# A planned encoder-layer kernel: nine instead of eight projection pairs by seven half products, in another order

## The chip, the core and the metric

The kernel runs on one core of a Trainium2 chip, as one program. The metric is the device time of one execution in microseconds (us). Before the change three runs took 727.42, 727.95 and 728.01 us; the median is 727.95. One further execution was profiled, and its trace gives all the durations used here.

A core has engines that run side by side, each with its own instruction stream: TensorE (PE; its weight loads are told apart as PEld), VectorE (DVE), ScalarE (ACT), GpSimd (POOL) and SyncE (SP, which only issues transfers). Sixteen DMA engines move the data.

## The reference: one encoder layer

Everything is float32. `x` has 512 tokens of 1024 features. The layer computes, with weights of some 68 MB in all:

```python
proj = x @ w_in                          # 1024 x 3840
qa, ka, va, qb, kb, vb = split(proj)     # 16 q heads, 4 k and v heads of 64; then 12 + 12 + 12
qa, ka, qb, kb = rope(...)               # first 16 of 64 dimensions turned by position
o_a = windowed attention(qa, ka, va)     # |i - j| <= 128, a sink logit per head, blocks of 128 queries
o_b = dilated mixture(qb, kb, vb)        # three groups of 4 heads: dilation 1, 4, 16; merged by softmax weight
g_a, g_b = sigmoid(x @ w_gate + b_gate)  # 1024 x 2048
y = (g_a * (o_a @ w_br_a) + g_b * (o_b @ w_br_b)) @ w_out
h = layer_norm(a * x + y)
out = layer_norm(a * h + (silu(h @ w_ff_gate) * (h @ w_ff_up)) @ w_ff_down)   # 1024 x 2816, twice, and back
```

## The kernel before

**Precision.** A float32 product is made of three fast products. Each operand is split into a high part (a cast) and a low part (the value less the high part); high x high, high x low and low x high are added in PSUM. So each 128-row slice of weights costs a load, a cast (on ACT or DVE, `cp_alts` or `copy_by_act`) and a subtraction on DVE, before TensorE takes three products.

**Dense units.** A unit is 128 output features: 8 slices of 128 inputs, three products of 512 columns each, 24 in all (`feat_x`, lines 523 to 525). Its weights come as two halves of 256 KB.

**Pairs.** `pair_x(ua, ub)` computes two units at once by Strassen's scheme in Winograd's form: seven products of half size instead of eight. The weights of both units form a 2 x 2 block matrix; blocks A11, A12 and A22 are loaded, S1 and S3 are loaded as sums (a plain load on SP's queue, and a second transfer on GpSimd's queue that adds to it), S2 and S4 are formed on DVE. All seven are split. The forms T1 to T4 of x are made once (`x_forms`, token `X`). Each product is 4 slices x 3 products of 256 columns (lines 639 to 641), so a pair has 84. ScalarE and VectorE take the results out of the banks.

**The planner.** Nothing is issued in the order of the text. `op(...)` notes an operation with what it reads and writes, the engines that can do it and a reckoned duration. `Program.run` then simulates all engines and at each moment gives a free engine the operation of lowest priority value whose inputs are there and whose buffers fit; this gives each engine's instruction order, which the chip then runs with semaphores. A priority is `pr.T`, the TensorE time noted so far, plus an offset: -130 for weights (`LOOK`), -100 for results out of banks (`EV`), so weights are sought 130 us ahead. `limits` counts buffers: 85 slots of 256 KB in classes (general, weights, attention), 8 PSUM banks, and `unit`, how many attention units may be under way at once. `SPARE` slots are kept free for the operation that is first in line.

**The order.** `ORDER` is a list of tokens. `VA` are the values of mixer A, `q1` to `q3` dense units of its queries, `P:a,b` a pair, `g` a gate, `R` turns the heads just computed by position (16 rows of each are gathered by DMA, four VectorE operations, and sent back), `A0` to `A3` the attention of mixer A (four blocks each), `Q00`, `K00` ... queries and keys of mixer B (head pair, group), `V0` and `V12` its values, `B0` to `B3` its four head slots, `O` fetches a slice of mixer A's output, `L` changes the weight buffers' limits, `X` makes the forms of x. Two gates are computed along with the first units.

**Gates.** There are 16; numbers 8 to 15 belong to mixer B and are computed first. `gate` makes one by a dense unit, `gate_of` takes one from a pair. `AWAY` holds 8 to 15: those made by a pair are stored in DRAM after the tanh (`put_away`) and fetched again after the last exponential of B3 (`fetch_gate`). `gate` does not store, so that gates 8 to 10 stay in their slots.

**After it.** When attention ends, the two branch products follow in the order `BRANCHES` (a0 to a4, b0, a5, ...), `gated` (line 1413) multiplies by the gates, then come the output product, the first layer norm, 22 blocks of the feed-forward net by half products (lines 1690 to 1692), its way back (1901 to 1903) and the last layer norm.

## Time and profile before

| what | value |
|---|---|
| median of three runs | 727.95 us (727.42 to 728.01) |
| span of the profiled execution | 725.8 us |
| TensorE busy | 717.3 us (99%) |
| VectorE busy | 655.6 us (90%) |
| ScalarE busy | 471.4 us (65%) |
| GpSimd busy | 134.0 us (18%) |
| moved by DMA | 140.3 MB, 193 GB/s |

The span goes from the first to the last instruction; the profile gives no other time for this execution, and the median of the runs is 2.15 us above it. A row of a group of instructions reads: line, engine, operation, what it writes `<-` what it reads (`sl` a slot, `ps` a PSUM bank, `x` the split x, `wpack` the weights, `gz` a gate in DRAM), shape, count | busy us, mean ns of one | idle time before them and who ended it. A row of the timeline reads: start in us, duration, engine, line, operation. Matmuls overlap: the duration of one is longer than the distance to the next.

### The profile page before, as it was taken

How to read it: one execution, taken by the hardware profiler on the slowest of the kernel's cores; microseconds unless marked ns; L12 is line 12 of the kernel's file. 1: busy time of each engine (PE TensorE's matmuls, PEld its weight loads, DVE VectorE, ACT ScalarE, POOL GpSimd, SP SyncE). 2: the span in 40 equal slices, each digit the busy share in tenths (PEclk: the TensorE clock that was granted, in tenths of full speed). 3: DMA queues.
4: the chain of work that ended last, by engine and by line, in shares of the span. 5: the costliest groups of instructions: out<-in, count | busy, mean ns of one | idle time of the engine just before them, and what ended most of it. 6: DMA issues, size and time to landing. Idle time of an engine off the chain costs nothing.

```text
span 725.8 us, 14412 instructions
## 1 busy us (share of the span) xinstructions
PE 717.3 (99%) x4767; PEld 666.2 (92%) x4767; DVE 655.6 (90%) x1408; ACT 471.4 (65%) x1077; POOL 134.0 (18%) x297
## 2 busy tenths in 40 slices
PE   9999999999999999999999999999999999999995
PEld 7889999989988888988888999999999999999985
DVE  6999999889997898898967898899999999899987
ACT  5757798868778665666534666756666566666821
POOL 0021211111100731450020021111112211212000
PEclk9999999999999999999999999999999999999998
DMA  8978788856577689965681499676888888979302
GB/s 256 309 155 202 191 213 246 211 135 172 170 192 185 160 228 253 309 217 185 216 209 44 116 267 228 154 199 155 200 254 212 193 215 225 258 184 200 97 30 87
DMA packets 88010, 140.30 MB, mean 193 GB/s; under 512 B 11136, under 2 KB 24064, under 8 KB 87936
## 3 DMA queue, kind: packets, MB, share of 16 engines
q1 hardware_dynamic: 74336, 114.87, 51.7%
q0 software_dynamic: 13328, 24.39, 20.5%
q8 instruction: 37, 0.61, 0.3%
q14 instruction: 37, 0.30, 0.1%
q10 hardware_dynamic: 272, 0.13, 0.1%
HBM read 114.97 MB, written 7.60 MB: 169 GB/s over the span
## 4 chain that ended last, share of the span: by engine, by line
PE 99%; DVE 1%; DVEq 0%; issue 0%
PE ps L1692 10%; PE ps L1691 9%; PE ps L1690 9%; PE ps L523 9%; PE ps L524 9%; PE ps L525 9%; PE ps L1901 4%; PE ps L1903 4%; PE ps L1902 4%; PE ps L641 3%; PE ps L640 3%; PE ps L639 3%; PE ps L973 3%; PE ps L1480 3%; PE ps L1481 3%; PE ps L1482 3%
## 5 line engine op out<-in xcount | busy, mean ns | idle before, releaser
L373 ACT ACTIVATE sl<-sl 128x512 fp32r<-128x512 f32 (+3 forms) x419 | 230.8, 583 | 59.7 <-DVE sl L544 31.1
L544 DVE TENSOR_TENSOR sl<-sl,sl 128x512 fp32r<-128x512 f32 (+3 forms) x378 | 222.4, 621 | 5.1 <-ACT sl L373 3.4
L373 ACT ACTIVATE sl<-ps 128x256 f32<-128x256 f32 (+5 forms) x209 | 88.7, 445 | 91.6 <-PE ps L1692 56.8
L387 POOL DMA_DIRECT2D sl<-wpack x60 | 53.1, 885 | 342.9 <-DMA sl<-wpack 118.2
L1691 PE MATMUL ps<-sl,sl 128*128 128x256 f32 x352 | 96.8, 275 | 0.0
L1692 PE MATMUL ps<-sl,sl 128*128 128x256 f32 x352 | 96.8, 275 | 0.0
L1690 PE MATMUL ps<-sl,sl 128*128 128x256 f32 x352 | 96.8, 275 | 0.0
L523 PE MATMUL ps<-x,sl 128*128 128x512 f32 (+1 forms) x241 | 93.9, 389 | 0.0
L525 PE MATMUL ps<-x,sl 128*128 128x512 f32 (+1 forms) x241 | 91.4, 379 | 0.0
L524 PE MATMUL ps<-x,sl 128*128 128x512 f32 (+1 forms) x209 | 79.5, 380 | 0.0
L1690 PE MATMUL ps<-x,sl 128*128 128x256 f32 x264 | 72.6, 275 | 0.0
L1691 PE MATMUL ps<-x,sl 128*128 128x256 f32 x264 | 72.6, 275 | 0.0
L1692 PE MATMUL ps<-x,sl 128*128 128x256 f32 x264 | 72.6, 275 | 0.0
L1691 PEld LDWEIGHTS ps<-sl,sl 128*128 128x128 f32 x352 | 67.6, 192 | 0.1
L1690 PEld LDWEIGHTS ps<-sl,sl 128*128 128x128 f32 x352 | 67.6, 192 | 0.1
L1692 PEld LDWEIGHTS ps<-sl,sl 128*128 128x128 f32 x352 | 67.6, 192 | 0.0
L399 DVE TENSOR_TENSOR sl<-sl,sl 128x512 fp32r<-128x512 f32 x94 | 62.8, 682 | 1.8 <-ACT sl L373 1.3
L525 PEld LDWEIGHTS ps<-x,sl 128*128 128x128 f32 x241 | 45.9, 190 | 6.5
L1690 PEld LDWEIGHTS ps<-x,sl 128*128 128x128 f32 x264 | 50.6, 192 | 0.4
L1691 PEld LDWEIGHTS ps<-x,sl 128*128 128x128 f32 x264 | 50.6, 192 | 0.4
L523 PEld LDWEIGHTS ps<-x,sl 128*128 128x128 f32 x241 | 46.0, 191 | 5.4 <-ACT sl L373 0.3
L1692 PEld LDWEIGHTS ps<-x,sl 128*128 128x128 f32 x264 | 50.7, 192 | 0.0
(172 smaller groups left out, 1851.0 us busy)
## 6 DMA issues: line engine op xcount, KB each, us to landing
sl<-wpack SPq DMA_DIRECT2D x249, 256.0 KB, 3.9
sl<-wpack POOLq DMA_DIRECT2D x60, 256.0 KB, 5.3
sl<-sl SPq DMA_DIRECT2D x110, 128.0 KB, 3.1
wf<-wpack SPq DMA_DIRECT2D x51, 256.0 KB, 5.2
wf<-wpack POOLq DMA_DIRECT2D x24, 256.0 KB, 6.2
oa<-sl SPq DMA_DIRECT2D x32, 128.0 KB, 3.6
sl<-sl SPq DMA_DIRECT2D x68, 32.0 KB, 2.6
sl<-oa SPq DMA_DIRECT2D x8, 256.0 KB, 5.1
```

The source lines that it names most:

```text
L373: nc.scalar.activation(dst, src, AF.Copy)
L387: op([(POOL, 1.0)], lambda e: nc.gpsimd.dma_start(b.t, src2, accum_op=ALU.add), reads=[b], writes=[b], prio=prio, moves=1.65)
L399: op([(DVE, dve(S))], lambda e: nc.vector.tensor_tensor(l.t, src.t, f32(h.t), op=ALU.subtract), reads=[src, h], writes=[l], prio=prio, abs ...
L523: mm(o, a, x0, start=(k == 0 and begins), stop=False, skip_group_check=split)
L524: mm(o, a, x1, start=False, stop=False, skip_group_check=split)
L525: mm(o, b, x0, start=False, stop=(k == nk - 1), skip_group_check=split)
L544: op([(DVE, dve(w))], lambda e: nc.vector.tensor_tensor(dst(), x(), y(), op=o), reads=reads, writes=writes, prio=prio)
L1690: mm(o, wh, pairs(bh[k]()), start=(first and k == 0), stop=False, skip_group_check=True)
L1691: mm(o, wh, pairs(bl[k]()), start=False, stop=False, skip_group_check=True)
L1692: mm(o, wl, pairs(bh[k]()), start=False, stop=(k == 3), skip_group_check=True)
L1901: mm(ps.t, x0, pairs(w[0].t), start=(first and m == 0), stop=False, skip_group_check=True)
L1902: mm(ps.t, x0, pairs(w[1].t), start=False, stop=False, skip_group_check=True)
```

## The change

One more pair: `Q10` and `K11`, dense units before, are computed by seven half products. The tokens of `ORDER` stand in another order, the other pairs are made of other units, and each token can carry an offset `@n` that is added to its priorities. Queries and keys are looked up by number, since they are no longer made in order. `gate` stores gates 8 to 15 in DRAM as well, so all eight go that way. Three attention units instead of two may be under way, ten instead of twelve slots are kept spare, the forms of x and the second values unit are ranked otherwise, and four fetches of mixer A's output wait for B1 instead of B0. The planner reckons the time until a transfer has landed 1.3 times as long as before, up to 380 us, and a transposition of four blocks 0.436 instead of 0.36 us.

The change also brings code that no token of the order calls: sums of a pair formed by DMA (`D:`), rows turned by DMA alone (`r`), values of mixer B by half products (`V`, `half_values`, `PV`) and sums of `unit_b` by DMA (`SUM_BY_DMA`, empty).

```diff
-SPARE, SPARE2 = 12, 12
+SPARE, SPARE2 = (10, 12)
...
-UNITS = 2
+UNITS = 3
...
+LONG = 1.3
...
 ORDER = """
-VA q1 A0 q2 q3 g X P:k1,q4 R A1 P:q5,g P:q6,q7 R A2 P:g,g A3 P:g,g L P:Q00,K00 R V12 P:Q01,K01 R P:Q02,K02 R V0 B0 Q10 K10 R Q11 K11 R B1 O O Q12 K12 R O O B2 B3 O O O O g8
+VA@-157 q2@22 q3@-17 g@46 X@-31 P:q6,q7@32 q1@-321 P:k1,q5@-23 R@-23 A1@-1 P:q4,Q02@-22 R@-13 V12@4 A0@-104 P:Q01,g@-19 A2@42 P:Q00,K00@8
+A3@-15 P:g,g@9 R@80 P:g,K01 R@-38 L@-65 P:g,K02 V0@33 R@2 P:Q10,K11@-27 R@-4 K10@1 Q12@-10 B0@-51 Q11@-32 B1@-2 O@11 R@-204 K12@-21 O@26 g@32
+R@31 O@-117 O@-34 g@-6 g@-45 g@-32 g@-9 B2@-102 O@-23 O@-77 g@-21 g@-1 B3@-47 g@-42 O@-172 O@-3
 """
-FORMS = -60.0
-VAL = -100.0
-OA_AFTER = (0, 0, 0, 0, 0, 0, 0, 0)
+FORMS = -135.0
+VAL = -130.0
+OA_AFTER = (0, 0, 0, 1, 1, 1, 0, 1)
...
+SUM_BY_DMA = ()
...
-                        o.done = moved + (LATE if 95 < now < 150 else 2.4 if 14 < now < SLOW else 0.87)
+                        o.done = moved + (LONG if now < 380 else 1.0) * (LATE if 95 < now < 150 else 2.4 if 14 < now < SLOW else 0.87)
...
-                        o.done = moved + (0.87 if e == ACT else 6.2 if ACC < now < 420 else 3.2 if 14 < now < SLOW else 2.2)
+                        o.done = moved + (LONG if now < 380 else 1.0) * (0.87 if e == ACT else 6.2 if ACC < now < 420 else 3.2 if 14 < now < SLOW else 2.2)
...
-        op([(PE, 0.36)], go, reads=[*toks, ident], writes=[pb])
+        op([(PE, 0.436)], go, reads=[*toks, ident], writes=[pb])
...
            halves(t.t), back(ps.t), AF.Tanh, bias=bg.t[:, f:f + 1], scale=0.5),
            reads=[ps, bg], writes=[t], prio=EV)
+        if f in AWAY:
+            put_away(f)
...
-                unit_a(g, b, qa[4 * g:4 * g + 4], ka[g], env["va"])
+                unit_a(g, b, qa[2 * g] + qa[2 * g + 1], ka[g // 2][g % 2], env["va"])
...
     for w in ORDER.split():
+        w, _, later = w.partition("@")
+        pr.T += float(later or 0)
         step(w)
+        pr.T -= float(later or 0)
```

More of the change, by code (lines that the diff above doesn't have):

```diff
@@ L607, in form @@
         def form(key, of, x, y):
+            if by_dma:
+                a, b = W[of], W[x if y == of else y]
+                op([(POOL, 1.0)], lambda e: nc.gpsimd.dma_start(a.t, b.t, accum_op=ALU.add), reads=[a, b], writes=[a],
+                   prio=-LOOK, moves=1.65)
+                W[key] = a
+                return
             tt(lambda: W[of].t, lambda: W[x].t, lambda: W[y].t, ALU.add, [W[x], W[y]], [W[of]], S, -LOOK)
@@ L714, in turn_rows @@
         g, h_ = (lambda: G.t[0:n]), (lambda: H.t[0:n])
-        op([(DVE, dve(S, extra=0.03))], lambda e: nc.vector.stream_shuffle(h_(), g(), SHUF2), reads=gs, writes=[H], prio=EV)
+        hs_ = [H]
+        if by_dma:
+            hs_ = []
+            for i, R in enumerate(tiles):
+                for h in range(2):
+                    for z in range(2):
+                        hs_.append((H, 4 * i + 2 * h + z))
+                        op([(SP, 0.1)], lambda e, R=R, i=i, h=h, z=z: nc.sync.dma_start(
+                            H.t[32 * i + 16 * h + 8 * z:32 * i + 16 * h + 8 * z + 8], R.t[64 * h + 8 - 8 * z:64 * h + 16 - 8 * z]),
+                           reads=[(R, 1), (R, 2)], writes=[hs_[-1]], prio=EV)
+        else:
+            op([(DVE, dve(S, extra=0.03))], lambda e: nc.vector.stream_shuffle(h_(), g(), SHUF2), reads=gs, writes=[H], prio=EV)
         op([(DVE, dve(S))], lambda e: nc.vector.tensor_tensor(g(), g(), c.t[0:n], op=ALU.mult),
@@ L880, in turned_values, with order @@
         for i in range(2):
+            if made:
+                t, z = slot(), made[i]
+                def order(e, t=t, z=z):
+                    s = z.t.rearrange("p (r t i) -> p t r i", r=4, t=nt)
+                    d = t.t.rearrange("p (t r i) -> p t r i", r=4, t=nt)
+                    copy(e, d[:, turn_by:], s[:, :nt - turn_by])
+                    copy(e, d[:, :turn_by], s[:, nt - turn_by:])
+                op([(ACT, act(S) + 0.1)], order, reads=[(z, 1), (z, 2)], writes=[t], prio=VAL if i else NORM)
+                src.append(t)
+                continue
             ps = done
```

191 lines of the change are left out of this document (171 added, 20 removed).

## The prediction

> **What bounds the kernel now.** I read the page's totals and its chain first, then the waits of TensorE alone.
>
> ```profile
> span 725.8 us, 14412 instructions
> ...
> PE 717.3 (99%) x4767; PEld 666.2 (92%) x4767; DVE 655.6 (90%) x1408; ACT 471.4 (65%) x1077; POOL 134.0 (18%) x297
> ...
> PE 99%; DVE 1%; DVEq 0%; issue 0%
> ```
>
> ```profile
> PE ps L459 <- DVE eps L510: 1.2, 1, 1.2
> ```
>
> The chain that ends last is TensorE almost throughout, and the list of TensorE's waits has one row, the 1.2 us before the warm-up products. But a busy TensorE is not yet one at its peak: the modelled ends overlap, so a short gap would be hidden. So I took the distance between starts, from two long stretches of the timeline (one of 256-column products, one of 512-column products, the first and last row of each) and their counts in the stretch table (stretch, TensorE, weight loads, VectorE, ScalarE, GpSimd busy, clock, DMA share, GB/s).
>
> ```profile
> 424.83 0.28 PE L1691 MATMUL ps<-sl,sl 128*128 128x256 f32 x1
> ...
> 474.97 0.28 PE L1690 MATMUL ps<-sl,sl 128*128 128x256 f32 x1
> ```
>
> ```profile
> 339.75 0.38 PE L523 MATMUL ps<-sl,sl 128*128 128x512 f32 x1
> ...
> 361.98 0.38 PE L524 MATMUL ps<-sl,sl 128*128 128x512 f32 x1
> ```
>
> ```profile
> 425.00:475.00 50.00, 50.00 (x450) 50.00 (x450) 45.07 (x90) 35.27 (x76) 9.76 (x12) 1.00 0.83 217
> ...
> 340.00:362.00 22.00, 22.00 (x104) 19.26 (x103) 21.88 (x37) 13.81 (x25) 0.86 (x1) 1.00 0.66 203
> ```
>
> (474.97 - 424.83) / 449 steps = 0.1117 us for a product of 256 columns; (361.98 - 339.75) / 103 = 0.2158 us for one of 512. The granted clock is 1.00 in both. The half products of the projections, which the change touches, run no slower: these two rows of one pair are twenty steps apart, 2.24 us, 0.112 each.
>
> ```profile
> 101.08 0.28 PE L639 MATMUL ps<-sl,sl 128*128 128x256 f32 x1
> ...
> 103.32 0.28 PE L641 MATMUL ps<-x,sl 128*128 128x256 f32 x1
> ```
>
> So TensorE is the bound, at its full rate, with nothing in between to win back. What remains is the amount of TensorE work, and the danger of putting gaps where there are none. That danger is read from the engine that feeds it:
>
> ```profile
> 25.00:50.00 25.00, 25.00 (x123) 21.93 (x122) 24.78 (x48) 17.99 (x36) 6.33 (x12) 1.00 0.86 228
> 50.00:75.00 25.00, 25.00 (x180) 23.74 (x180) 24.08 (x54) 18.01 (x44) 3.83 (x7) 1.00 0.75 185
> 75.00:100.00 25.00, 25.00 (x216) 24.72 (x215) 23.99 (x55) 20.75 (x50) 4.36 (x8) 1.00 0.80 200
> 100.00:125.00 25.00, 25.00 (x210) 24.53 (x209) 23.70 (x55) 22.71 (x56) 3.96 (x14) 1.00 0.83 237
> ...
> 225.00:250.00 25.00, 25.00 (x141) 22.39 (x140) 21.49 (x66) 19.01 (x56) 10.85 (x46) 1.00 0.63 170
> 250.00:275.00 25.00, 25.00 (x134) 22.23 (x133) 21.54 (x57) 16.56 (x37) 10.13 (x27) 1.00 0.89 227
> 275.00:300.00 25.00, 25.00 (x143) 22.51 (x142) 20.95 (x56) 12.76 (x34) 4.07 (x8) 1.00 0.98 267
> 300.00:325.00 25.00, 25.00 (x137) 22.31 (x136) 23.09 (x67) 18.56 (x50) 17.29 (x65) 1.00 0.79 268
> 325.00:350.00 25.00, 25.00 (x133) 22.30 (x132) 22.85 (x45) 14.59 (x31) 0.00 (x0) 1.00 0.57 182
> ```
>
> From 25 to 125 us VectorE has 0.22 + 0.92 + 1.01 + 1.30 = 3.45 us free in all, though TensorE never waits for it; from 225 to 300 us it has 3.51 + 3.46 + 4.05 = 11.0 us.
>
> **The change part by part.** *The ninth pair.* In the old order Q10 and K11 are two dense units; in the new one they are a pair. Counting the other tokens of both orders gives the same work: the old pairs hold k1 and q4 to q7, six of the Q and K, and five gates, the new ones these same and Q10 and K11; VA, q1 to q3, V0, V12, nine gates one by one, A0 to A3, B0 to B3 and eight O stand in both; both have eight R over 17 tiles in all. So TensorE loses two dense units, 2 x 8 x 3 = 48 products of 512 columns, 48 x 0.2158 = 10.36 us, and gains a pair, 7 x 12 = 84 products of 256 columns, 84 x 0.1117 = 9.38 us: 0.98 us less. As TensorE has no idle time, all of it is on the path.
>
> By the Trainium skill (TensorE: Matmul & The Clock Gate, Back-to-back issue gap) a stream of weight loads and products sustains 81 ns at 128 columns and 131 ns at 512. An estimate from these figures, on a straight line, is 98 ns at 256: the pair would cost 84 x 0.098 = 8.2 us against 48 x 0.131 = 6.3 us, so the change would lose 1.9 us. This trace disagrees: it has 111.7 and 215.8 ns, where the same section's formula for products by themselves gives 109 and 216.
>
> *What the pair asks of the others.* Rows of the page (instruction groups: busy, mean ns) and of the lines that empty the pair's banks (count, shortest/median/longest ns):
>
> ```profile
> L373 ACT ACTIVATE sl<-sl 128x512 fp32r<-128x512 f32 (+3 forms) x419 | 230.8, 583 | 59.7 <-DVE sl L544 31.1
> L544 DVE TENSOR_TENSOR sl<-sl,sl 128x512 fp32r<-128x512 f32 (+3 forms) x378 | 222.4, 621 | 5.1 <-ACT sl L373 3.4
> ...
> L1691 PEld LDWEIGHTS ps<-sl,sl 128*128 128x128 f32 x352 | 67.6, 192 | 0.1
> ```
>
> ```profile
> L662 DVE SCALAR_TENSOR_TENSOR sl<-ps,sl x8: 409/420/425, 67.8 to 191.2; 128x256 f32<-128x256 f32 x8
> ```
>
> Two dense units split four half weights: 4 x 0.62 = 2.5 us of VectorE. A pair splits seven, forms two sums, adds one wide result and one half result: (7 + 2 + 1) x 0.62 + 0.42 = 6.6 us. That is 4.1 us more VectorE; on ScalarE three more casts, 3 x 0.58 = 1.7 us, and small copies either way. Placed after V0, this lies in the stretch with 11.0 us free, so I cost it at nothing. Without that cover up to 4.1 us would go to TensorE.
>
> *Transfers.* A pair reads five half weights plainly and adds two by GpSimd's queue; two dense units read four. Queue rows (packets, MB, share of 16 engines' span) and issues up to 340 us (size, median us to landing):
>
> ```profile
> q1 hardware_dynamic: 74336, 114.87, 51.7%
> q0 software_dynamic: 13328, 24.39, 20.5%
> ```
>
> ```profile
> sl<-wpack SPq DMA_DIRECT2D x129, 256.0 KB, 3.9
> ...
> sl<-wpack POOLq DMA_DIRECT2D x16, 256.0 KB, 4.8
> ...
> gz<-sl SPq DMA_DIRECT2D x5, 256.0 KB, 4.0
> ```
>
> A plain MB takes 0.517 x 725.8 / 114.87 = 3.27 us of all engines, an added one 0.205 x 725.8 / 24.39 = 6.1. One plain and two added halves of 0.262 MB: 0.9 + 3.2 = 4.1 us. Three more gates stored and fetched: 6 x 0.262 x 3.27 = 5.1 us. From 225 to 350 us the engines have (0.37 + 0.11 + 0.02 + 0.21 + 0.43) x 25 = 28.5 us free, so the sum fits, but hardly between 250 and 300. On GpSimd each addition waits for its plain load, and behind it in order stand other additions and the small copies of the attention units. GpSimd has over 14 us free in each 25 from 225 to 300. Bounds: nothing, or the landing of the two in series, 2 x 4.8 = 9.6 us, if their operand were needed at once; weights are ranked 130 us ahead of their use, so nothing.
>
> *All of gates 8 to 15 by way of DRAM.* Old: gates 8, 9 and 10 stay in their slots. New: they too are stored after the tanh, in SP's queue among the weight loads, and fetched after the last exponential of B3. Cost of six issues on SP: 6 x 0.33 us (row below), hidden by its idle time. What is late next would be b0's gated product on VectorE. First and last fetch, its landing, and that product today (the one just ahead of the first sum of gates):
>
> ```profile
> L1401 SPq DMA_DIRECT2D sl<-gz x5: 326/327/381, 337.5 to 355.9; - x5
> ...
> DMA to landing us min/median/max: 2.6/3.6/5.3
> ```
>
> ```profile
> 341.67 0.68 DVE L1413 SCALAR_TENSOR_TENSOR sl<-sl,ps 128x512 f32<-128x512 f32 x1
> ```
>
> If gate 8 were fetched no earlier than the first is now, it would land between 337.5 + 2.6 = 340.1 and 342.8: up to 1.1 us late, gates 9 and 10 a little more. Behind it VectorE would hold its other gated products and splits, and TensorE would wait for their banks. I take nothing: the order is planned with 2.5 us of transfer for each, so b0 can stand later. Upper end 3 us.
>
> *Other order, three units of attention at once, two spare slots less, transfers reckoned 1.3 times as long.* None adds an instruction; each moves them. The three early pairs become q6/q7, k1/q5 and q4/Q02, V12 comes after three pairs instead of six, and A0 after it. V12 is dense work of 96 x 0.2158 = 20.7 us with eight splits of VectorE, 5 us: an earlier relief. Against that, X and the first pair come before A0, whose scores filled TensorE meanwhile. Bounds: a gain of at most the gaps that exist (the span less TensorE's 717.3 is 8.5 us: 1.2 is the wait above, 7.3 the end behind the last product, so only gaps hidden under overlapping ends are left, up to 0.16 us each), a loss of some operations of VectorE, 0.62 us each. I take 0. "Longer reckoned" touches only the plan; real transfers stay. The branches for sums by DMA, for values by half products and for rows turned by DMA are defined and not called.
>
> **The sum.** The profiled execution has a span of 725.8 us; the median of the runs is 727.95, and I take the 2.15 between them as what lies around the span, unchanged. 727.95 - 0.98 = 726.97. Nothing else changes TensorE's work; ahead of it and behind it stays what is there (last product, last VectorE operation):
>
> ```profile
> 718.26 0.23 PE ps L1482
> ...
> 722.15 0.40 DVE sl L1543
> ```
>
> About 0.2% (1.46 us) is what a measurement of this kernel can tell from no change, so 726.5 to 729.4 counts as the same, and the forecast lies in it.
>
> **The rivals.** *Short gaps eat it.* A new order with VectorE at 95% and more leaves places where a weight is ready just as it is needed. One to three operations late, 0.6 to 1.9 us: 727.6 to 728.9. For it: 3.45 us free in 100. Against: the old order had the same 95% there and not one wait that the view shows.
>
> *VectorE becomes the bound.* The mechanism: pairs need 6.6 us of VectorE plus their rotations in 9.4 us of TensorE; where pairs, the forms of x and attention meet, the 4.1 us more push the later splits back and TensorE waits the rest. In full: 726.97 + 4.1 = 731.1. It is slower (over 729.4) from the point at which 2.4 of the 4.1 us find no free time, that is under 1.7 us free around the added pair. For it: the rows from 25 to 125 us. Against: 11.0 us free where the pair stands.
>
> *The fetch of gate 8 is late at b0.* Up to 3 us: at most 730.0; slower from 2.4 us on.
>
> *A half product costs more than half.* Both widths need one weight load each, and from 425 to 475 us the loads are busy all 50.00 us, so the load may set the pace. Break-even is 10.36 / 84 = 0.123 us a product; were a load's 192 ns not overlapped at all, the pair would take 84 x 0.192 = 16.1 us: 727.95 + 5.8 = 733.7. Against it stand the rows at 101 and 103 us: 0.112 in a pair. The Trainium skill's sustained figures, named above, would put it at about 729.9 by the same estimate.
>
> *A gain over 0.2%.* It needs 0.5 us beyond the 0.98, from gaps that the views don't show.
>
> **How the numbers follow.** Forecast without new gaps (726.4 to 727.5): 0.56. Short gaps (727.5 to 729.4): 0.18. VectorE the bound: 0.14. Gate 8 late: 0.05, counted as slower. Half product dearer: 0.01, slower. Faster by over 0.2%: 0.06. So faster 0.06, same 0.56 + 0.18 = 0.74, slower 0.14 + 0.05 + 0.01 = 0.20. The range, 726.4 to 729.8, leaves out most of the slower cases and nearly all of the fast one.
>
> **What would show it.** Right: 48 products fewer at lines 523 to 525 of the old numbering and 84 more at the pair's three, TensorE's waits still one row, its span down by 1.0 us. VectorE's free time from 225 to 300 us falls by some 4 us. Eight stores and eight fetches of gates. Wrong would be: a wait of TensorE for a split or a cast between 30 and 130 us or around the ninth pair (VectorE the bound), one for a bank behind the gated products near 340 us (gate 8), or a stretch of half products with more than 0.112 us between starts.

## The result and the profile after

| kernel | median | range | runs |
|---|---|---|---|
| before | 727.98 us | 727.42 to 728.41 | 4 |
| changed | 736.05 us | 735.57 to 737.57 | 4 |

The ratio is 1.0113 (95% interval 1.0097 to 1.0130): slower by 8.1 us, outside the range of 726.4 to 729.8. The profiled execution of the changed kernel took 735.57 us, with a span of 733.8 against 725.8. In the experiments below, two executions of the run "replan, SP 0.63", of 746.41 and 1530.16 us, ran in a slower state of the core and are left out.

From the page of the changed kernel: totals, the two large DMA queues (packets, MB, share of 16 engines), and the chain that ends last.

```profile
span 733.8 us, 14483 instructions
...
PE 719.4 (98%) x4803; PEld 666.4 (91%) x4803; DVE 657.0 (90%) x1405; ACT 474.7 (65%) x1092; POOL 138.4 (19%) x299
...
q1 hardware_dynamic: 75344, 116.71, 52.3%
q0 software_dynamic: 13616, 24.91, 20.5%
...
PE 96%; DVE 2%; DMA 1%; ACT 1%; issue 0%; SPq 0%; DVEq 0%; ACTq 0%
```

TensorE has 4803 products against 4767: 36 more, 84 less 48, as reckoned. The queues moved 1.84 MB more plainly and 0.52 MB more by addition, as the pair and the gates ask (0.26 + 1.57, and 0.52). VectorE is busy 1.4 us and ScalarE 3.3 us longer. But TensorE's idle time, span less busy, rose from 725.8 - 717.3 = 8.5 us to 733.8 - 719.4 = 14.4. Its busy time rose too, by 2.1 us, although its products cost 0.98 us less: the modelled ends hide short gaps. 5.9 + 2.1 = 8.0 us is the whole difference of the spans. Nothing was added to TensorE's work; it waits.

The waits of TensorE (engine, what it does, what it waited for: total, times, longest), seven rows where there was one before; the four longest:

```profile
PE ps L1385 <- DVE sl L952: 1.3, 1, 1.3
PE ps L463 <- DVE eps L514: 1.2, 1, 1.2
PE ps L1218 <- DVE sl L1156: 1.2, 2, 0.7
PE ps L527 <- DVE st L1283: 1.1, 1, 1.1
...
```

The stretches (TensorE, weight loads, VectorE, ScalarE, GpSimd busy, clock, DMA share, GB/s) say where:

```profile
125.00:150.00 25.00, 23.01 (x145) 20.27 (x144) 18.20 (x50) 17.92 (x46) 3.58 (x9) 1.00 0.84 207
...
250.00:275.00 25.00, 25.00 (x137) 22.14 (x136) 23.46 (x67) 16.64 (x48) 11.18 (x27) 1.00 0.85 214
275.00:300.00 25.00, 21.36 (x120) 18.45 (x119) 16.59 (x52) 14.40 (x41) 7.42 (x21) 1.00 0.95 244
```

In the kernel before, the first of these stretches reads (the one from 275 us stands in the prediction, with TensorE at 25.00 and VectorE at 20.95):

```profile
125.00:150.00 25.00, 25.00 (x170) 23.22 (x169) 21.15 (x51) 18.11 (x46) 4.59 (x10) 1.00 0.72 183
```

Two holes: 2.0 us in 125 to 150 and 3.6 us in 275 to 300, as far as the modelled ends show them. VectorE is not the bound in either: it falls there from 21.15 and 20.95 to 18.20 and 16.59 us, so it waits along with TensorE. The first hole ends, and the second begins, like this (timeline: start, duration, engine, line, what; idle time and its end):

```profile
145.33 0.87 ACT L377 ACTIVATE sl<-ps 128x256 fp32r<-128x256 f32 x2 [3.74 <-PE ps L650]
145.80 0.42 DVE L952 TENSOR_TENSOR sl<-ps,sl 128x256 fp32r<-128x256 f32 x1 [2.82 <-ACT sl L377]
...
146.25 0.48 PE L1217 MATMUL ps<-sl,sl 128*128 128x512 f32 x1 [0.83 <-ACT sl L377]
```

```profile
268.67 15.41 SPq L832 DMA_DIRECT2D sl<-sl  x16
```

```profile
281.20 0.69 DVE L403 TENSOR_TENSOR sl<-sl,sl 128x512 fp32r<-128x512 f32 x1 [1.95 <-DMA sl<-sl]
...
282.28 0.96 PE L1385 MATMUL ps<-sl,sl 128*128 128x256 f32 x5 [1.29 <-DVE sl L952]
```

In the second, a split on VectorE (line 403) waits by its row 1.95 us for a transfer from slot to slot, a move of heads between partitions that still uses the slot it writes; line 952, the split of the values that TensorE needs, stands behind it in order. SP's sixteen moves of heads of queries and keys take 15.4 us just then; their issues are some 8.7 us of it (16 with a median of 0.54), for the rest SP waits itself. This accounts for 1.3 of the 3.6 us. The larger part of the second hole, 2.3 us, lies between 290 and 300 us, where VectorE stands 3.0 us (row below) behind a product that was long done; what really ended that wait is not shown.

```profile
295.17 0.42 DVE L1280 TENSOR_TENSOR sl<-ps,sl 128x256 f32<-128x256 f32 x1 [3.00 <-PE ps L1273]
```

In the first, ScalarE's row names a product that was long done, so by the reading rule it was something else; a store of an attention output (line 1224) landed at about that moment, 7.4 us after its issue, the longest of its group. That ScalarE waited for this store fits the time, and fits the relief below, but no row says it:

```profile
L1224 SPq DMA_DIRECT2D oa<-sl x3: 580/607/624, 136.4 to 137.8; - x3
...
DMA to landing us min/median/max: 4.2/4.6/7.4
```

### The profile page after: what moved, and what is told of

Same layout as the page of the kernel before. It is cut to its first block, busy times and chain, and to the rows that moved or that the text cites. A ratio compares the mean times of both kernels' runs of the same rounds, so it can differ in the third digit from the quotient of the medians.

```text
span 733.8 us, 14483 instructions
## 1 busy us (share of the span) xinstructions
PE 719.4 (98%) x4803; PEld 666.4 (91%) x4803; DVE 657.0 (90%) x1405; ACT 474.7 (65%) x1092; POOL 138.4 (19%) x299
## 4 chain that ended last, share of the span: by engine, by line
PE 96%; DVE 2%; DMA 1%; ACT 1%; issue 0%; SPq 0%; DVEq 0%; ACTq 0%
PE ps L1894 9%; PE ps L1896 9%; PE ps L1895 9%; PE ps L527 8%; PE ps L528 8%; PE ps L529 8%; PE ps L651 4%; PE ps L650 4%; PE ps L649 4%; PE ps L2105 4%; PE ps L2107 4%; PE ps L2106 4%; PE ps L1151 3%; PE ps L1686 3%; PE ps L1685 3%; PE ps L1684 3%
## 5 line engine op out<-in xcount | busy, mean ns | idle before, releaser
L377 ACT ACTIVATE sl<-sl 128x512 fp32r<-128x512 f32 (+3 forms) x427 | 235.0, 584 | 65.7 <-DVE sl L548 42.5
L548 DVE TENSOR_TENSOR sl<-sl,sl 128x512 fp32r<-128x512 f32 (+3 forms) x387 | 227.1, 622 | 3.1 <-ACT sl L377 2.4
L377 ACT ACTIVATE sl<-ps 128x256 f32<-128x256 f32 (+7 forms) x213 | 88.0, 437 | 85.0 <-PE ps L1896 53.0
L527 PE MATMUL ps<-x,sl 128*128 128x512 f32 (+1 forms) x225 | 87.5, 389 | 1.1 <-DVE st L1283 1.1
L529 PE MATMUL ps<-x,sl 128*128 128x512 f32 (+1 forms) x225 | 85.2, 379 | 0.0
L528 PE MATMUL ps<-x,sl 128*128 128x512 f32 (+1 forms) x193 | 73.4, 380 | 0.0
L403 DVE TENSOR_TENSOR sl<-sl,sl 128x512 fp32r<-128x512 f32 x90 | 60.3, 683 | 7.5 <-ACT sl L377 4.7
L548 DVE TENSOR_TENSOR sl<-sl,ps 128x512 f32<-128x512 f32 (+1 forms) x68 | 44.5, 659 | 9.5 <-PE ps L2107 5.4
L1895 PEld LDWEIGHTS ps<-x,sl 128*128 128x128 f32 x264 | 50.6, 192 | 0.4
L1894 PEld LDWEIGHTS ps<-x,sl 128*128 128x128 f32 x264 | 50.6, 192 | 0.4
L1896 PEld LDWEIGHTS ps<-x,sl 128*128 128x128 f32 x264 | 50.7, 192 | 0.0
L527 PEld LDWEIGHTS ps<-x,sl 128*128 128x128 f32 x225 | 42.9, 191 | 6.4 <-issue 1.3
```

The source lines that it names most:

```text
L377: nc.scalar.activation(dst, src, AF.Copy)
L403: op([(DVE, dve(S))], lambda e: nc.vector.tensor_tensor(l.t, src.t, f32(h.t), op=ALU.subtract), reads=[src, h], writes=[l], prio=prio, abs ...
L527: mm(o, a, x0, start=(k == 0 and begins), stop=False, skip_group_check=split)
L528: mm(o, a, x1, start=False, stop=False, skip_group_check=split)
L529: mm(o, b, x0, start=False, stop=(k == nk - 1), skip_group_check=split)
L548: op([(DVE, dve(w))], lambda e: nc.vector.tensor_tensor(dst(), x(), y(), op=o), reads=reads, writes=writes, prio=prio)
```

## The experiments

The theories: **Q**, SP's in-order queue issues too late; **B**, the bytes on the DMA engines make small transfers land late; **P**, GpSimd stands in order behind additions that wait for a fetch; **S**, too few spare slots. Deltas are (ratio - 1) x 727.9, against the kernel before on the same chip; the changed kernel itself has +8.2.

| run | from | median | ratio (95%) | delta |
|---|---|---|---|---|
| stores by GpSimd | changed, same plan | 732.65 | 1.0062 (1.0040, 1.0084) | +4.5 |
| no additions | changed, same plan | 730.58 | 1.0033 (1.0019, 1.0047) | +2.4 |
| small additions | changed, same plan | 731.98 | 1.0046 (1.0028, 1.0064) | +3.3 |
| both reliefs | changed, same plan | 731.34 | 1.0049 (1.0035, 1.0063) | +3.6 |
| SP reckoned 0.65 | changed | 737.37 | 1.0120 (1.0090, 1.0150) | +8.7 |
| all parts, new order | changed | 733.03 | 1.0071 (1.0056, 1.0086) | +5.2 |
| true turns | before | 728.00 | 1.0000 (0.9989, 1.0011) | 0.0 |
| gates away | before | 731.45 | 1.0048 (1.0028, 1.0068) | +3.5 |
| three units | before | 733.14 | 1.0068 (1.0052, 1.0083) | +4.9 |
| ten spare slots | before | 731.77 | 1.0056 (1.0041, 1.0071) | +4.1 |
| ninth pair alone | before | 729.82 | 1.0029 (1.0018, 1.0041) | +2.1 |
| replan, SP 0.63 | before | 728.70 | 1.0009 (0.9999, 1.0019) | +0.7 |
| replan, bias | before | 728.83 | 1.0016 (1.0005, 1.0027) | +1.2 |
| 24 tiny transfers | before, same plan | 730.48 | 1.0029 (1.0014, 1.0043) | +2.1 |
| 24 of 128 KB | before, same plan | 732.13 | 1.0057 (1.0037, 1.0077) | +4.1 |
| ten spare, small additions | before | 728.46 | 1.0009 (0.9996, 1.0023) | +0.7 |
| gates away, small additions | before | 728.92 | 1.0009 (0.9999, 1.0018) | +0.7 |
| pair, stores by GpSimd | before | 730.82 | 1.0041 (1.0029, 1.0054) | +3.0 |

### Reliefs of the changed kernel at an untouched plan

The engine that issues the stores of attention outputs (line 1224):

```diff
-            op([(SP, 0.73)], lambda e, part=part: nc.sync.dma_start(
+            op([(SP, 0.73)], lambda e, part=part: nc.gpsimd.dma_start(
...
```

> The changed kernel with its plan untouched (same order on every engine, all of the change kept), but the 32 stores of the attention units' outputs to DRAM are issued from GpSimd's queue instead of SP's. Theory Q (SP's queue: from 180 to 290 us its issues of some 0.64 us each follow one another without room, so the moves of heads between partitions are issued and land late and the engines that work in order stand): 32 x 0.64 = 20 us of SP's time go, TensorE's gap of 5.4 us between 275 and 300 us shrinks to under 1.5, and the time falls from 736 to between 728 and 732. Theory B (the engines that carry the transfers are the limit, with the additions into fetched O at 258 to 280 us): the bytes are the same, so 735 to 737. Theory S (too few spare slots: results wait for slots whose last store has not landed, the gap of 2.9 us at 131 to 148 us): the stores land no earlier, that gap stays, and the later one too.

The additions into fetched O left out, and then kept but small (line 1505):

```diff
-        op([(POOL, 1.0)], lambda e: nc.gpsimd.dma_start(st.t, src(1), accum_op=ALU.add), ...
+        op([(POOL, 1.0)], lambda e: None, ...
```

> The changed kernel with its plan untouched, but the eight DMAs that add the second half of O (the products with the low parts of the values) to the fetched first half are left out, so the low-order part of O is missing from the output. Theory B: 2 MB of added transfers go, the gap of 5.4 us between 275 and 300 us goes with them, 730 to 732; the gap of 2.9 us at 131 to 148 us stays. Theory Q: SP issues as many transfers as before and the late moves stay late, 734.5 to 736.5. Theory S: as Q.

```diff
-        ... lambda e: nc.gpsimd.dma_start(st.t, src(1), accum_op=ALU.add), ...
+        ... lambda e: nc.gpsimd.dma_start(st.t[0:16], src(1)[0:16], accum_op=ALU.add), ...
```

> The changed kernel with its plan untouched; the eight additions into fetched O are kept as instructions on GpSimd, with their wait for the plain fetch, but each adds 16 of the 128 rows, so the low-order part of O is missing for the other rows. Leaving the additions out gave 730.6 us. Theory B (the engines that carry the transfers are the limit): seven eighths of the bytes are gone, so 730 to 732. A new theory P (GpSimd is blocked: its additions wait up to 13 us for the plain fetch, and the statistics and the clearing of the score tiles of the next attention units stand behind them in order): the wait is still there, so 734.5 to 737. Theory Q (SP's issues): nothing changes on SP, 735 to 737.

Both edits together:

> The changed kernel with its plan untouched and both reliefs at once: the 32 stores of the attention outputs issued by GpSimd's queue instead of SP's, and the eight additions into fetched O on 16 of 128 rows only (the low-order part of O is missing for the rest). The stores alone gave 732.7, the additions alone 732.0. Theory T (two separate places where small transfers land late, one behind SP's queue at 131 to 148 us, one behind the bytes of the O fetch at 255 to 300 us): the gains add, 736.05 - 3.4 - 4.1 = 728.5, between 727.5 and 729.5, and TensorE's gaps between 125 and 300 us sum to under 2.5 us. If one resource explained all, both reliefs would overlap: 731 to 732.

The stretches from 125, 250 and 275 us of the kernel with the stores on GpSimd's queue:

```profile
125.00:150.00 25.00, 25.00 (x166) 23.00 (x165) 21.63 (x58) 20.81 (x55) 7.92 (x19) 1.00 0.76 201
...
250.00:275.00 25.00, 23.08 (x125) 19.89 (x124) 22.90 (x66) 15.26 (x44) 13.90 (x39) 1.00 0.83 201
275.00:300.00 25.00, 23.82 (x140) 21.23 (x139) 19.63 (x65) 17.48 (x52) 8.79 (x28) 1.00 0.98 266
```

and of the kernel with small additions:

```profile
125.00:150.00 25.00, 23.47 (x145) 20.54 (x144) 19.08 (x51) 17.00 (x43) 3.41 (x10) 1.00 0.83 210
...
250.00:275.00 25.00, 24.93 (x134) 21.55 (x133) 21.10 (x60) 17.56 (x48) 10.21 (x31) 1.00 0.78 214
275.00:300.00 25.00, 25.00 (x147) 22.68 (x146) 21.51 (x69) 17.39 (x51) 13.01 (x40) 1.00 0.93 254
```

The first relief closes the first hole (25.00) and only moves the second about; the second relief closes the second hole (25.00, from 21.36) and leaves three quarters of the first (23.47); its trace has 1.1 us of idle time more between 200 and 225 us. Taking seven eighths of the added bytes away, while GpSimd still waits for the fetch of O (row below), gives 8.2 - 3.3 = 4.9 us back; taking the additions out altogether gives 5.8. So the bytes make most of the second hole (B). GpSimd's blocking (P) is not cleanly apart from them: its second group of additions also goes out earlier with small additions, at 294.05 instead of 297.00 us.

```profile
266.43 1.58 POOL L1505 DMA_DIRECT2D sl<-oa  x2 [13.66 <-DMA sl<-oa]
```

Moves of heads, 128 KB each, landed a median 5.7 us after issue from 250 to 300 us in the changed kernel, 4.6 with small additions, 3.3 with none (what it writes `<-` what it reads, issuing queue, count, size, median us to landing):

```profile
sl<-sl SPq DMA_DIRECT2D x24, 128.0 KB, 5.7
```

```profile
sl<-sl SPq DMA_DIRECT2D x25, 128.0 KB, 4.6
```

```profile
sl<-sl SPq DMA_DIRECT2D x24, 128.0 KB, 3.3
```

My theory that the two reliefs add (728.5) fell: together they give 731.34, no better than one of them. The Trainium skill (DMA: Bandwidth & Descriptors, Issuing engines are not separate DMA queues) says that all engines' transfers end on the same sixteen DMA engines, and that another issuing engine saves only sequencer time. The trace agrees as far as the engines' load goes: with the stores on GpSimd the DMA share from 275 to 300 us stayed high, at 0.98 after 0.95. Why the two do not add is not shown by this alone.

The profile of both reliefs shows where part of the remaining loss lies: its span is 4.5 us above the kernel before. TensorE is idle for 2.2 us between 150 and 275 us, 1.5 of it in the stretch from 250 us, waiting for normalised probabilities (line 1139). Shortly behind that gap its granted clock falls to a half (the first products behind it, then two stretches of 2.5 us):

```profile
260.10 2.05 PE L1151 MATMUL ps<-ident,sl 128*128 128x128 f32 x8 [1.44 <-ACT sl L1139]
```

```profile
260.00:262.50 2.50, 2.33 (x11) 1.79 (x12) 2.50 (x9) 2.50 (x8) 2.00 (x3) 0.74 0.71 235
262.50:265.00 2.50, 2.50 (x9) 1.99 (x9) 2.50 (x7) 1.68 (x5) 2.09 (x7) 0.58 0.51 94
```

(0.26 + 0.42) x 2.5 = 1.7 us is an estimate of what the slower clock cost. In the changed kernel's own profile the clock is 1.00 through this part.

The planner told the truth about SP:

```diff
-                        end = now + (0.62 if 14 < now < SLOW else 0.47)
+                        end = now + (0.65 if 14 < now < SLOW else 0.47)
```

> The changed kernel planned anew with one number changed: an issue on SP reckoned at 0.65 us instead of 0.62, the distance that the trace shows. The plan itself then has a gap of 0.74 us at 174 us and ends 0.73 us later. Theory Q: the plan no longer orders more than SP can issue, the lag of some 11 us at 280 us goes and with it most of the gaps: 728 to 731. Theories B and P: the moves are issued as late and land as late as before, 734 to 738.

It came out at 737.37, no better than the changed kernel, where Q foretold 728 to 731. It is also a new plan, with holes at other places, so this speaks against Q as the single cause and does not settle it.

### One part of the change alone

Transposes reckoned as in the changed kernel (the same in two further places, and 0.218 for 0.18 in a fourth), in the kernel before:

```diff
-        op([(PE, 0.36)], go, reads=[*toks, ident], writes=[pb])
+        op([(PE, 0.436)], go, reads=[*toks, ident], writes=[pb])
...
```

> The kernel before with one number of its planner changed: the transposes are reckoned at 0.436 us (0.218 for a half one) instead of 0.36, as in the changed kernel; in the plan itself TensorE then still has no gap beyond the first 6 us. Theory Q with its second half (the short reckoning made the planned TensorE run ahead of the real one by up to 4.9 us at 280 us, which was slack for SP's lag of up to 10 us; the truthful one takes it away): gaps of 2 to 6 us appear between 225 and 300 us, 730 to 734. If that slack was not what kept the old order whole: 727.4 to 728.6, no gap. Theories B and S say nothing of this kernel beyond 728.

728.0, ratio 1.0000, and one row of waits as before. The idea that too short a reckoning had been the old plan's slack fell.

All of gates 8 to 15 by way of DRAM. The edit is in `gate`, so it is the gates made by a dense unit that are now stored as well; the expectation names them wrongly as those made in pairs.

```diff
            reads=[ps, bg], writes=[t], prio=EV)
+        if f in AWAY:
+            put_away(f)
```

> The kernel before with one part of the change alone: the gates made in pairs are stored to DRAM too, so all of gates 8 to 15 go by way of DRAM, six SP issues more. My prediction's price of this part is nothing, with up to 3 us if the fetch of gate 8 is late: 727.4 to 728.6 expected by all theories; 729 to 731 with a wait near 340 us if gate 8 is late; a gap before 300 us would speak for theory Q, as six issues more on SP's queue would then be enough to make one.

```diff
-UNITS = 2
+UNITS = 3
```

> The kernel before with one number changed: three attention units may be begun at once instead of two. The plan itself has no gap of TensorE after 6 us. Theory M (any part that lets the plan use up the time between a transfer's landing and its use costs on the chip, where landings scatter): 729 to 733, with gaps behind moves of heads. If the parts are harmless by themselves and only the new order of the projections matters: 727.4 to 728.6.

```diff
-SPARE, SPARE2 = 12, 12
+SPARE, SPARE2 = 10, 12
```

> The kernel before with one number changed: ten spare slots kept back for operations that finish something instead of twelve. No gap of TensorE after 6 us in the plan. Theory S (results that wait for slots) and theory M both: 729 to 733; with S the waits stand at writes into slots whose last transfer has not landed. If the parts are harmless by themselves: 727.4 to 728.6.

Each of these three, which my prediction costed at nothing, cost 3.5 to 4.9 us alone. They add up to 12.5, more than the whole change lost, so they are not a sum. Ten spare slots and the gates open their hole between 300 and 325 us; three units open theirs between 275 and 300 us (2.9 us) and a smaller one behind it (1.2 us). Two rows of the three units' waits from 270 to 284 us:

```profile
ACT sl L373 <- DMA sl<-oa: 4.1, 1, 4.1
...
PE ps L973 <- ACT sl L961: 2.6, 1, 2.6
```

ScalarE stands 4.1 us before a cast of a fetched O (line 373), whose addition was issued at 271.60 us and ends 7.9 us later on the chain; the normalising of probabilities (line 961) stands behind it in order, and TensorE waits 2.6 us for that. From 282.5 to 285.7 us its granted clock is then 0.50, which cost some 1.7 us by the same estimate as above. So here too a late fetch of O has an engine in order behind it, ScalarE this time; no relief was tried.

The ninth pair alone (the tokens from `L` on, and the code that reads the offsets; the rest as before). In this order the output comes out with other values (a relative error of 0.24), which I did not trace to a line, so its time is that of a kernel that does not compute the layer; products, VectorE and ScalarE operations are as many as in the changed kernel (4803, 1405, 1092).

```diff
-... L P:Q00,K00 R V12 P:Q01,K01 R P:Q02,K02 R V0 B0 Q10 K10 R Q11 K11 R B1 O O Q12 K12 R O O B2 B3 O O O O g8
+... L@-95 P:Q00,K00 V12@10 R@-15 P:Q01,K01@10 R@-20 P:Q02,K02@10
+R@-115 V0@40 P:Q10,K10@-15 R@10 K11@-10 B0@-30 R@-5 O B1@-30 Q11@-25 Q12@10 K12 O@-15 O@-40 O@15 O@40 R g8 O@40 B2 O@5 O@95 B3@-80
```

> The kernel before with one part of the change alone, the ninth pair (Q10 with K10 here), and nothing else of it: its transfers, gates, units, spare slots and transposes are reckoned and placed as before; only the tokens from L on are ordered anew, so that the plan has no gap of TensorE after 6 us. My prediction's own step: 48 x 0.2158 - 84 x 0.1117 = 0.98 us less, 726.9 to 727.2, if the parts other than the pair made the loss. If the ninth pair's own transfers (0.26 MB plain, 0.52 MB added, three issues) bring the stalls: 729 to 733, with gaps between 200 and 320 us.

From its page:

```profile
PE 715.6 (98%) x4803; PEld 666.2 (92%) x4803; DVE 656.1 (90%) x1405; ACT 477.0 (66%) x1092; POOL 133.9 (18%) x299
```

TensorE's busy time fell by 1.7 us, so the saving is there; but the span is 727.7, so 3.6 us of idle time came with it, and the kernel lost 2.1 us in all. Most of this idle time has nothing to do with the projections. The start of the last product, before and with the pair:

```profile
718.10 0.38 PE L1482 MATMUL ps<-sl,sl 128*128 128x512 f32 x1
```

```profile
718.29 0.38 PE L1486 MATMUL ps<-sl,sl 128*128 128x512 f32 x1
```

TensorE ends only 0.2 us later than before. What follows takes 727.7 - 718.67 = 9.0 us instead of 725.8 - 718.48 = 7.3, since VectorE has two blocks of the last layer norm to finish there instead of one: 1.7 of the span's 1.9 us. Three new waits of TensorE make the rest and use up the saving: 0.5 us at the start (line 524), 0.8 in the first layer norm (line 1565), and 0.4 at 275 to 300 us (line 1200). Whether the pair or its order made the end of the plan another is not shown.

### Is it just any new plan?

Two neutral numbers of the kernel before, so that only the plan differs:

```diff
-                        end = now + (0.62 if 14 < now < SLOW else 0.47)
+                        end = now + (0.63 if 14 < now < SLOW else 0.47)
```

> The kernel before with no part of the change: only an issue on SP is reckoned at 0.63 us instead of 0.62, so the whole is planned anew, other in places from 100 us on, with no gap of TensorE after 6 us in the plan. Theory F (the fit: the old plan is one whose late transfers happen not to reach TensorE, and most other plans of the same work lose 2 to 5 us): 729.5 to 733. Theory D (the parts of the change cost by what they ask for or take away): 727.3 to 728.6.

```diff
-BIAS = 0.2
+BIAS = 0.22
```

> As the run with 0.63 us on SP, another neutral number: the bias by which the planner prefers ScalarE to VectorE is 0.22 instead of 0.20. Planned anew from 5 us on; the plan ends 0.2 us later, with 0.3 us more of gaps. Theory F: 729.5 to 733. Theory D: 727.5 to 728.8.

0.7 us, which is within the noise, and 1.2 (0.4 to 2.0): a new plan as such costs little, not 3.5 to 4.9. With the true turns, also a new plan, at 0.0, theory F (the old plan is a rare lucky one) explains at most a third of such an effect here; three plans are few.

### How much room the kernel before has

Twenty-four further transfers behind the moves of keys, of one row of 64 numbers (shown), and of 64 rows of 512:

```diff
...
+                        if key == "d":
...
+                            nc.sync.dma_start(scr[0][len(scr) - 2], f32(z.t[a:a + 1, 0:64]))
...
```

> The kernel before, plan untouched, with 24 additional transfers of 256 bytes, each issued by SP right behind a move of a key's heads (there are 48 such moves between some 190 and 295 us): 24 issues more and no bytes to speak of. Theory Q: 24 x 0.64 = 15 us of SP's time in a stretch where the changed kernel has some 9 issues more; TensorE gets gaps between 200 and 320 us, 731 to 737. Theory B: no bytes, 727.5 to 728.8. Theory P: no addition waits longer unless SP is late, so as Q if the plain fetches of O are issued later, else as B.

> As the kernel with 24 additional tiny transfers, but each carries 128 KB: 24 issues and 3.1 MB more, 3.1 x 3.27 = 10 us of all engines by the kernel before's own rate, which is about twice what the change adds before 340 us. The difference to the tiny ones is the price of bytes alone. Theory B: 4 to 10 us above the tiny ones. Theory Q: within 1.5 us of the tiny ones, since the issues are the same.

+2.1 and +4.1 us. Issues alone cost 2.1 us, for some 13 us of SP's time (24 at about 0.54 us in the trace); 3.1 MB cost another 2.0, less than the 4 to 10 that pure B foretold. Both kinds of room are short, and neither is gone.

### The shared cause of two parts

The kernels with ten spare slots and with the gates away, each with the additions on 16 of 128 rows:

> The kernel before with ten spare slots, plan untouched, and the eight additions into fetched O on 16 of 128 rows only (the low-order part of O is missing for the rest). Ten spare slots alone took 731.8 (+4.2), with 5.6 us of gaps between 300 and 325 us behind GpSimd's wait of 14.4 us for a fetch of O. Theory B (bytes of the O fetch make transfers late): 727.5 to 729, gaps at 300 to 325 us under 1.5. Theory P (GpSimd's statistics stand in order behind additions that wait for the plain fetch, however small): 730.5 to 732. Theory S (slots): 730.5 to 732.

> The same for the kernel before with all of gates 8 to 15 by way of DRAM (731.45, +3.6, gaps of 3.9 us between 300 and 325 us behind a wait of GpSimd of 13.2 us for a fetch of O): the additions on 16 of 128 rows only, plan untouched. Theory B: 727.5 to 729. Theory P: 730 to 732. If the gates' own transfers make it: 730 to 732 too, with GpSimd's wait shorter.

Both came back to +0.7 us (728.46 and 728.92). What links the additions to TensorE is seen on GpSimd's timeline and in the stretch from 300 to 325 us. In order: ten spare slots; gates away; gates away with small additions; ten spare slots with small additions.

```profile
294.40 3.53 POOL L1308 DMA_DIRECT2D sl<-oa  x4 [14.43 <-DMA sl<-oa]
297.98 0.18 POOL L1118 COPY st<-st 32x2 f32<-32x2 f32 x1
```

```profile
293.02 3.53 POOL L1310 DMA_DIRECT2D sl<-oa  x4 [13.15 <-DMA sl<-oa]
296.60 0.18 POOL L1118 COPY st<-st 32x2 f32<-32x2 f32 x1
```

```profile
291.43 2.33 POOL L1310 DMA_DIRECT2D sl<-oa  x3 [11.77 <-DMA sl<-oa]
...
295.72 0.18 POOL L1118 COPY st<-st 32x2 f32<-32x2 f32 x1
```

```profile
290.23 3.11 POOL L1308 DMA_DIRECT2D sl<-oa  x4 [10.40 <-issue]
293.39 0.18 POOL L1118 COPY st<-st 32x2 f32<-32x2 f32 x1
```

That stretch, in the same order (columns as above):

```profile
300.00:325.00 25.00, 22.14 (x110) 18.42 (x109) 17.86 (x47) 16.25 (x39) 14.08 (x55) 0.93 0.77 247
```

```profile
300.00:325.00 25.00, 22.42 (x119) 18.82 (x119) 18.55 (x48) 17.00 (x40) 13.66 (x50) 1.00 0.81 268
```

```profile
300.00:325.00 25.00, 23.15 (x122) 19.50 (x122) 19.05 (x49) 17.16 (x40) 12.74 (x48) 1.00 0.64 210
```

```profile
300.00:325.00 25.00, 24.37 (x135) 21.38 (x134) 21.04 (x52) 18.33 (x41) 10.50 (x39) 1.00 0.51 171
```

GpSimd begins the statistics of two attention units (line 1118) at 297.98, 296.60, 295.72 and 293.39 us, as soon as its additions are out; TensorE's idle time is 2.86, 2.58, 1.85 and 0.63 us. Within each plan, earlier statistics make a smaller hole. So B and P work together: the fetch of O comes late, its addition blocks GpSimd in order, the statistics behind it hold up the probabilities, and TensorE waits (its rows name lines 961 and 998, the normalising and the split). With small additions SP issues these fetches 2.5 us (ten slots) and 1.9 us (gates) earlier; their time to landing fell only in the first, from a median 7.5 to 5.8 us, and not in the second (5.9, then 6.1). So what moved them is mostly when SP gets to them. With ten slots the clock adds to it: it is 0.93 in the stretch above, 0.50 from 311.5 to 314.5 us right behind the gap, some 1.7 us lost by the estimate used above.

Between plans the rule does not hold. In the kernel before, GpSimd also stands long before its additions (13.94 us until 285.86 us), and the statistics begin later than in all four, without any hole (TensorE 25.00 in this stretch):

```profile
299.15 0.86 POOL L1308 DMA_DIRECT2D sl<-oa  x1 [2.91 <-DMA sl<-oa]
300.05 0.63 POOL L1118 COPY st<-st 32x2 f32<-32x2 f32 x1
```

There the first transposition of these probabilities (line 973) comes at 313.11 us in TensorE's order, 13.1 us after the statistics began, and does not wait. With ten slots it starts at 311.29 us, 13.3 us after the statistics, and with the gates at 310.18, 13.6 after, both after a wait; so the new plans put it where it needs statistics some microseconds earlier than they came. In the old plan the additions go out one or two at a time, not three or four.

### Looking for a better version

The pair alone with the stores by GpSimd, with one fetch of O placed elsewhere in the order, and the changed kernel in another order (shown; it takes the place of the whole `ORDER`):

```diff
+VA q1 A0 q2 q3 g X P:k1,q4 R A1 P:q5,g P:q6,q7 R@10 A2 P:g,g@-5 P:g,g@10 L@-50 A3@-40 P:Q00,K00 V12@10 R@-75 P:Q01,K01@10 R@-25 P:Q02,K02@-30 R@-110
+P:Q10,K10@-55 R@20 K11@5 R@-5 V0@40 B0@-60 B1@-10 O@-20 Q12@10 O@-25 K12 Q11@-35 O@-50 O@70 R@-10 g8@5 O@60 O@20 B2@-30 O@-20 O@110 B3@-45
```

> The kernel before with the ninth pair alone (Q10 with K10, the tokens from L on ordered anew, the fifth fetch of O behind the last gates), and the 32 stores of the attention outputs issued by GpSimd's queue instead of SP's with the plan unchanged. The pair alone took 729.8; the relief of SP's queue gave the changed kernel 3.4 us. If the pair's remaining stalls stand behind SP: 727.0 to 728. If not, or if the stores delay GpSimd's statistics: 729 to 731.

> The changed kernel with every number and part of it kept, but the projections, values and attention units in another order (the old kernel's early part, Q10 with K10 as ninth pair), found so that the plan has hardly a gap also when SP's issues are reckoned longer and the transfers slower. The plan ends 0.14 us later than the changed kernel's. If the order with its late rotations made the loss: 727.5 to 730. If the parts make it, whatever the order: 732 to 737. Theory F has 729.5 to 733 for any plan.

Neither beats the kernel before. The first (its output has other values, as that of the pair alone) is no faster than the pair alone, 3.0 against 2.1 us; since its order differs in a fetch of O too, what the stores cost or free there is not shown. The second, at +5.2, recovers 3 of the 8.2 us, so the order has a share, but the parts keep the larger one; its hole is now at 200 to 225 us, and the longest of TensorE's waits there is one of a pair (line 648) for ScalarE:

```profile
200.00:225.00 25.00, 22.16 (x162) 20.20 (x161) 20.84 (x50) 17.05 (x44) 1.57 (x8) 1.00 0.74 208
```

```profile
PE ps L648 <- ACT sl L656: 2.3, 2, 1.7
```

## Why the prediction was wrong

- **TensorE the bound, at full rate, no gap before.** Right: 36 products more, clock 1.00 in the changed kernel's profile, and what it lost there is waits of TensorE.
- **The ninth pair saves 0.98 us on the path.** The work fell as reckoned, the time did not: the pair alone cost 2.1 us. Its profile puts 1.7 us of the loss behind the last product, in the last layer norm, and only 0.4 us of its new waits where the transfers crowd; the other output values and the other order leave open what the pair itself does to the time.
- **More VectorE, ScalarE and DMA time, hidden.** VectorE and ScalarE: hidden, as forecast, if not in size (VectorE 1.4 us more instead of 4.1, ScalarE 3.3 instead of 1.7); the rival "VectorE becomes the bound" did not happen. DMA: a flaw. I summed the free shares of the DMA engines from 225 to 350 us (28.5 us) against 9.2 us asked, as if a transfer late by some microseconds cost nothing as long as the total fits. My own row had 0.98 in 275 to 300.
- **Gates by way of DRAM: "hidden by its idle time", upper end 3 us at b0.** Wrong in place and price: 3.5 us alone, and not at b0 (340 us) but at 300 to 325 us, behind the fetch of O.
- **"Other order, three units of attention at once, two spare slots less ... I take 0."** This is the step that failed. I bounded what moves by single VectorE operations of 0.62 us. Three units cost 4.9 and spare slots 4.1 us alone, and what moved were transfers against the work that needs them: moves of heads and fetches of O that come a few microseconds too late for the new plan, with in-order engines behind them.
- **"Longer reckoned touches only the plan."** True turns, the reckoning that I could test alone, were 0.0. `LONG` was not tried alone.
- **The rivals.** None named the right mechanism, a late transfer with an in-order engine behind it. "Short gaps eat it" was nearest in kind, but I sized a gap by one to three VectorE operations (at most 728.9).

Shown: in the changed kernel the loss is TensorE waiting; two of the parts alone lose through late fetches of O and GpSimd's order, and return to +0.7 us when most of the added bytes go; in the whole change the hole at 275 to 300 us closes with these bytes, the one at 125 to 150 us when the stores leave SP's queue. Seen in a trace, with no experiment on it: three units lose behind a late fetch of O with ScalarE in order behind it, and a gap can bring 1.7 us more by a halved clock. Open: why the two reliefs do not add, what ends VectorE's wait at 295 us in the changed kernel, and what the ninth pair would cost in an order with the right output. That two units and twelve spare slots were room for late landings is argued, not shown.

## What to carry to other kernels

Where TensorE is at 99% because an order written ahead of time has every transfer land in time, a change is priced by what it does to landings, and not only by what it adds to engines: find the stretches with the highest DMA share (0.89 and 0.98 here, from 250 to 300 us of the kernel before), list which engines wait there in order for a transfer (here SP for moves, GpSimd for additions, ScalarE for casts of what was fetched), and ask what TensorE has to do if each comes a few microseconds late. A limit that keeps slots or units back may be slack for those landings, so try each part alone first; here three "free" ones cost 3.5 to 4.9 us each.

## What the hardware showed that I had not expected

- The landing of one and the same 128 KB move between partitions depends on the crowd: in the kernel before a median of 2.4 us from 200 to 250 us, and 6.2 from 250 to 300.

```profile
sl<-sl SPq DMA_DIRECT2D x30, 128.0 KB, 2.4
```

```profile
sl<-sl SPq DMA_DIRECT2D x26, 128.0 KB, 6.2
```

  The Trainium skill (DMA: Bandwidth & Descriptors, Anatomy of one DMA) gives, for a transfer that GpSimd issues, about 2.0 us and the bytes at 436 GB/s, an estimate of 2.3 us. These moves were issued by SP, so it is not the same path: the 2.4 us are close to that figure, and the 6.2 us are 3.9 us above it.

- SP took 0.63 us from one move to the next in a train: eight of 128 KB in 5.03 us in the changed kernel. Other transfers came closer together: four weight loads of 256 KB in 1.98 us, and the 256-byte transfers some 0.54 us each. Twenty-four of the latter cost the kernel 2.1 us. The Trainium skill (DMA: Bandwidth & Descriptors, Issuing engines are not separate DMA queues) calls the issuing time usually small beside the transfer; for such a train it is not, as each of these eight landed 2.3 us after its issue while the issues took 5.0.

```profile
215.93 5.03 SPq L877 DMA_DIRECT2D sl<-sl  x8
```

- A gap of TensorE can cost more than its length. In four traces (ten spare slots, three units, both reliefs, SP reckoned 0.65) TensorE ran at a granted clock of 0.50 for some 3 us, from at most 1.5 us behind gaps with waits of 2.6, 2.6, 1.4 and 1.7 us; a product of 512 columns then took 0.43 us from start to start instead of 0.216. The cost is 1.7 us each, estimated from the clock. In the kernel with the gates away a wait of 1.8 us was not followed by it, so the length of the last gap alone does not decide it.

```profile
311.50:314.50 3.00, 3.00 (x12) 2.33 (x11) 2.38 (x6) 2.25 (x6) 2.63 (x11) 0.50 1.05 388
```
